# A Mamba-2 and attention trunk on one core: softmax weights turned in 32x32 blocks on VectorE and regrouped through DRAM

## The chip, the core and the metric

One core of one Trainium2 chip runs the whole program. The metric is the device time of one execution in microseconds (us); lower is better. Engines are named as in the profile: PE (TensorE, matrix multiply), PEld (its weight loads), DVE (VectorE), ACT (ScalarE), POOL (GpSimd) and SP (SyncE, which here only issues DMAs). Instructions are said to read "128x512" when 128 partitions hold 512 elements each.

## The reference, cut to what matters

256 positions of width 2048 pass through one Mamba-2 layer, then one causal attention layer with 16 heads of width 128, then a final RMSNorm. Everything is float32.

```python
def reference(x, ...):
    h = rmsnorm(x, a_norm_g)
    x = x + mamba2_layer(h, ...)             # one projection to 10304 columns: z, x, B, C and 64 columns dt
    kb, vb, kbar = shared_kv(x, kv_norm_g, w_kv)
    h = rmsnorm(x, b_norm_g)
    x = x + moba_layer(h, b_w_in, b_w_out, kb, vb, kbar)
    return rmsnorm(x, final_norm_g)

def moba_layer(h, w_in, w_out, kb, vb, kbar):
    proj = h @ w_in                          # 2048 columns of queries, 2048 of gates
    q, z = rope(proj[..., :2048]), proj[..., 2048:]
    o = softmax(causal(q @ k.T * scale)) @ v # per head; 256 positions are one block
    return (o * silu(z)) @ w_out
```

## The kernel before, in words

**The main stream on PE.** All projections are cut into blocks of 512 output columns, and a block into units of 256 input rows. A unit loads a 128x1024 piece of float32 weights (`load`, on SP's queue), splits it into a rounded part `hi` (ACT) and a rest `lo` (DVE, both in `split`), and multiplies: for each of two groups of 128 positions and two groups of 128 input rows three matmuls of 512 columns (`products`), so 12 matmuls in a unit and 96 in a block. They accumulate in four PSUM banks (`ps`). There are 384 such units and one odd one, `dt`, whose weights have 64 columns: 16 pairs of matmuls with the activations as the moving operand, `hi` over 512 columns and `lo` over 256.

**The turn.** A block of queries, gates or convolution channels leaves PSUM with positions on the partitions and is wanted with channels there. `turn` (L385) transposes in 32x32 blocks on DVE (`T`), SP writes `T` to DRAM (`turned`), and four DMAs on POOL's queue read it back regrouped (`U`).

**The side work.** Everything else (convolution, state-space part, norms, attention) is written as Python generators that a planner steps between the products: `some` (L156) takes a step of one whose inputs are due by the planner's own clock, `Side.advance` books when the next is due, and `copied` (L257) books a trip through DRAM as 5.0 us for the write, 0.6 us for each of four issues and 7.0 us for the read. A step is taken only while ACT and DVE stand less than an allowance ahead of PE in that clock: at most 1000 ns, and less near a block's end (`left`, `LAG_END`, `CATCH_UP`). The result is a fixed order on each engine; at run time engines wait only for data.

**Attention.** `att_gen` (L994) handles two heads, eight times in all. It applies rope to the queries, has PE form scores (`K,q`), and on DVE and ACT turns them into normalized weights `E` (tile `Es`, 128x2x384, two buffers), positions on the partitions. The weights must then be transposed: PE does it with the identity, three 128x128 pieces for each head into a PSUM bank `s`, and ACT copies them to `W` (tile `PT`). Four matmuls of `W` with the values follow (`PT,V`), then the gate. The heads come from blocks in the order `z0 q0 z1 q1 z2 q2 q3 z3` (q queries, z gates; L1100). The blocks of the last projection read the gated heads.

**The start and the end.** Before the first data arrive PE runs three 128x512 float32 matmuls on a tile of ones (`warm_up`, L496: one, a 16-column transpose, two). Then `h_gen` transposes x piece by piece, ACT and DVE make the operand `hT`, and the first products follow. At the end `last_evac` (L1134) adds the last products of 128 positions to x, squares, forms the root on 128x1 tiles (`root`, L475), scales four pieces of 512 columns and writes each.

Of the kernel before, what the change touches and what calls it, by code (L numbers as in the profile page):

```python
# [15 lines left out]
P = 128  # L16
L = 256
# [12 lines left out]
LAG = 1000.0  # L30
LAG_END = 0.0
CATCH_UP = 0.3
MARGIN = 750.0
# [98 lines left out]
class Side:  # L132


    def __init__(self, clock, engines, lag):
        self.gens, self.clock, self.engines, self.lag = [], clock, engines, lag

# [3 lines left out]
    def advance(self, entry):  # L141
        gen, ready, _ = entry
        if ready is not None and not ready():
            return 0
        before = [e.ns for e in self.engines]
        at = 0.0
        try:
            entry[1] = next(gen)
            if isinstance(entry[1], float):
                at, entry[1] = entry[1], None  # L150
        except StopIteration:
            self.gens.remove(entry)
        entry[2] = max([e.ns for e, b in zip(self.engines, before) if e.ns > b], default=at)
        return 1

    def some(self, most):  # L156


        PE = self.engines[0]
        for entry in list(self.gens):  # L160
            if most <= 0 or any(e.ns > PE.ns + self.lag() for e in self.engines):
                return
            if entry[2] <= PE.ns - MARGIN:
                most -= self.advance(entry)
# [7 lines left out]
def trunk_kernel(ctx: ExitStack, tc: tile.TileContext, x, a_norm_g, a_w_in, a_conv_w, a_conv_b,  # L172
# [47 lines left out]

    left = [0.0]
    side = Side(clock, [PE, ACT, DVE], lambda: min(LAG, LAG_END + CATCH_UP * (left[0] - PE.ns)))

# [90 lines left out]
    def split(u):  # L314
# [5 lines left out]
        t = RAW.pop(u)  # L320
        shape = [P, 16, 64] if b["form"] == "dt" else [P, 2, 512]
        hi = wts.tile(shape, F32R, name="hi", tag="hi", bufs=HI_BUFS)
        lo = wts.tile(shape, F32R, name="lo", tag="lo", bufs=HI_BUFS)
        HI[u], LO[u] = hi, lo
        if j == 0:
# [17 lines left out]
    def products(u):  # L343
        b, k, row = units[u]
        acc = accs.setdefault(id(b), {})
        hi, lo, k0, k1 = HI.pop(u), LO.pop(u), b["ks"][0], b["ks"][-1]
        last = k + 1 == k1
        if b["form"] == "dt":
            ps = bank("ps_dt")
            for i in range(16):  # L350
                for w, n in ((hi, 2 * L), (lo, L)):
                    PE.matmul(ps[0:64, :n], lhsT=w[:, i, :], rhs=b["operand"](i)[:, :n],
                              start=i == 0 and w is hi, stop=i == 15 and w is lo)
            b["evac"](ps[0:64, :])
            some(4)
            return
        rows = (0, 1) if row is None else (row,)
        for j in rows:
# [15 lines left out]
            some(2)  # L374

    def halves(ps):

        t = take("T")[:ps.shape[0], :L]
        ACT.activation(t, ps[:, L:2 * L], AF.Copy)
        S[0].give((t.tensor.name, t.offset))  # L380
        return ps[:, :L], t

# [109 lines left out]
    early = big.tile([P, 2, 1024], F32, name="early", tag="y6")  # L492
    DVE.memset(early[:, 0, 512:], 1.0)
    warm = take("s")

    def warm_up(n):  # L496
        for _ in range(n):
            PE.matmul(warm, lhsT=early[:, 0, 512:512 + P], rhs=early[:, 0, 512:], start=True, stop=True)

    warm_up(1)  # L500
    g_a = const.tile([P, 16], F32, name="g_a")
# [3 lines left out]
    banks.give((pa.tensor.name, pa.offset))  # L505
    warm_up(2)
    banks.give((warm.tensor.name, warm.offset))
    nt = const.tile([P, 4, 2], F32, name="r0")
# [61 lines left out]
    def dt_evac(ps):  # L570
        a, t = halves(ps)
        w = big.tile([P, 5, L], F32, name="dtw", tag="y7")
        v = w[0:64, 0, :]
        DVE.tensor_add(v, a, t)
        make_room("s")
        p = take("s")[:, :L]
        for i in range(2):
            PE.transpose(p[:, i * P:(i + 1) * P], r0[:, i:i + 1].to_broadcast([P, P]), ident)
        DVE.tensor_mul(v, v, p[0:64])
        give(p)  # L580
        DVE.tensor_scalar(v, v, dta[:, 0:1], None, op0=OP.add)
        side.add(dt_gen(w))

    def dt_gen(w):
# [30 lines left out]
        DVE.tensor_copy(b[64:128, :], a)  # L615
        DVE.tensor_copy(b[0:64, :], dt)
        yield can("s")
        p = take("s")[:, :L].rearrange("p (t c) -> p t c", t=2)
# [375 lines left out]
    def att_gen(half, there, h0):  # L994
# [38 lines left out]
        W = take("PT")  # L1033
        for e in range(2):
            yield can("s")
            T = take("s")[:, :384]
            for i in range(3):
                PE.transpose(T[:, i * P:(i + 1) * P], E[:, e, i * P:(i + 1) * P], ident)
            yield
            ACT.activation(W[:, e, :], T, AF.Copy)  # L1040
            give(T)
        give(E, m)
        yield can("s")
        o = take("s").rearrange("p (e l) -> p e l", e=2)
# [83 lines left out]
    def fin_part():  # L1128

        p = B["p"].tile([P, 2], F32, name="part", bufs=1)  # L1130
        DVE.tensor_reduce(p, ss[:, :, 0:3], axis=mybir.AxisListType.X, op=OP.add)
        B["part"] = p

    def last_evac(ps, t):  # L1134
        if t == 0:
            fin_part()
        v, gf = fin_add(3, t, ps), B["gf"]

        w = B["p"].tile([P, 4, 1], F32, name="sfin", bufs=2)
        DVE.tensor_add(w[:, 0, :], ss[:, t, 3:4], B["part"][:, t:t + 1])  # L1140
        root(w, D)
        r = w[:, 2, :]
        o = B["x1"][t]
        for c in (0, 512):
            ACT.activation(o[:, c:c + 512], o[:, c:c + 512], AF.Copy, scale=r)
        DVE.tensor_scalar(o[:, 1024:1536], o[:, 1024:1536], r, None, op0=OP.mult)
        DVE.scalar_tensor_tensor(v, v, r, gf[:, 1536:], op0=OP.mult, op1=OP.mult)
        for c in (1024, 0, 1536, 512):
            SP.dma_start(dram(out, t * P * D + c, [[D, P], [1, 512]]), o[:, c:c + 512])

# [15 lines left out]
    for i in range(2):  # L1166
        next(prep)
        part(i)
    next(prep)
    load(4)  # L1170
    begun = 1
    for u in range(len(units)):
# [18 lines left out]
        if u == first_p + 12:  # L1191
            open_b()
        rest = (b["ks"][-1] + 1 - k) * (0.32e3 if b["form"] == "dt" else 1.36e3) * (0.5 if b["form"] == "rows" else 1.0)
        left[0] = PE.ns + rest
        products(u)
# [43 lines left out]
```

## Time and profile before

| what | value |
|---|---|
| median of three runs | 1151.7 us (1150.7 to 1152.11) |
| the profiled execution's own time | 1152.41 us |
| its span, first to last instruction | 1150.3 us |
| PE busy | 1137.7 us, 99% |
| DVE, ACT, POOL busy | 835.0 us, 646.7 us, 106.6 us |
| HBM traffic | 232.69 MB read, 18.94 MB written |
| granted TensorE clock, mean | 0.997 of full |

Every wrapped instruction is recorded at one line (L128), so groups are told apart by their tiles: `s<-ident,Es` is a transpose of the weights `Es` into a bank `s`. A matmul's recorded duration contains its pipeline, and the next one begins before it ends; what a matmul costs PE is the distance between starts, which the chain of waits shows. The chain follows the work that ended last back from the end.

### The profile page before, as it was taken

To read this page: it belongs to the slowest core of one execution; us is meant where nothing else is said; L and a number is where in the kernel's file an instruction comes from. 1 tells how busy PE (TensorE), PEld (TensorE's weight loads), DVE (VectorE), ACT (ScalarE), POOL (GpSimd) and SP (SyncE) were. 2 spreads that over 40 slices of the span, in tenths; PEclk is the share of its full clock that TensorE was granted. 3 is DMA by queue.
4 is the path that set the end of the run, shared out by engine and by line. 5 is a ranking of instruction groups with operands and counts; after the bars stand their busy time and mean duration, and the time that the engine had idled before them with its cause. 6 is when DMAs were issued, how large, how long until landed. Compare 5 with 4: busy or idle time off the path is not lost.

```text
span 1150.3 us, 14948 instructions
## 1 busy us (share of the span) xinstructions
PE 1137.7 (99%) x5281; PEld 929.9 (81%) x5281; DVE 835.0 (73%) x1274; ACT 646.7 (56%) x904; POOL 106.6 (9%) x185
## 2 busy tenths in 40 slices
PE   9999999999999999999999999999999999999996
PEld 6778888888888888888878888888888888888885
DVE  5876868787888978787877569876444676677564
ACT  5656566666676566757654655434444354544453
POOL 2011111012011111101000000010000001000000
PEclk9999999999999999999999999999999999999998
DMA  8777879878677778877765457678567677667552
GB/s 261 232 228 218 264 223 282 267 247 256 218 219 238 205 233 237 237 224 234 224 227 168 164 185 234 205 243 257 176 213 229 200 222 227 198 212 239 165 183 91
DMA packets 127674, 252.61 MB, mean 220 GB/s; under 512 B 12336, under 2 KB 12416, under 8 KB 127216
## 3 DMA queue, kind: packets, MB, share of 16 engines
q1 hardware_dynamic: 118080, 222.86, 62.5%
q0 software_dynamic: 9520, 28.81, 9.5%
q8 instruction: 41, 0.67, 0.2%
q14 instruction: 33, 0.27, 0.1%
HBM read 232.69 MB, written 18.94 MB: 219 GB/s over the span
## 4 chain that ended last, share of the span: by engine, by line
PE 99%; DVE 0%; ACT 0%; issue 0%; ACTq 0%
PE ps L128 91%; PE s L128 7%; PE ps_dt L128 0%; ACT hi L128 0%; DVE lo L128 0%; DVE sfin L128 0%; ACT T L128 0%; ACT x L128 0%; DVE x L128 0%; ACTq L1234 0%; DVE dtw L128 0%; DVE early L128 0%; ACT hT L128 0%; ACT sfin L128 0%; DVE ones L128 0%
## 5 line engine op out<-in xcount | busy, mean ns | idle before, releaser
L128 DVE TENSOR_TENSOR lo<-raw,hi 128x1024 fp32r<-128x1024 f32 (+1 forms) x385 | 463.4, 1217 | 196.8 <-ACT hi L128 193.5
L128 ACT ACTIVATE hi<-raw 128x1024 fp32r<-128x1024 f32 (+1 forms) x385 | 397.1, 1052 | 260.1 <-PE ps L128 145.9
L128 PE MATMUL ps<-hi,hT 128*128 128x512 f32 x1280 | 400.7, 394 | 0.7 <-ACT hi L128 0.7
L128 PEld LDWEIGHTS ps<-hi,hT 128*128 128x128 f32 x1280 | 235.7, 188 | 49.2 <-issue 2.2
L128 PE MATMUL ps<-lo,hT 128*128 128x512 f32 x640 | 249.8, 390 | 0.0
L128 PE MATMUL ps<-hi,bop 128*128 128x512 f32 x512 | 160.4, 394 | 0.0
L128 PE MATMUL ps<-hi,yn 128*128 128x512 f32 x512 | 159.7, 393 | 0.0
L128 PE MATMUL ps<-hi,kvop 128*128 128x512 f32 x512 | 158.1, 390 | 0.0
L406 POOL DMA_DIRECT2D U<-turned x128 | 74.1, 586 | 823.1 <-DMA turned<-T 557.2
L128 PEld LDWEIGHTS ps<-lo,hT 128*128 128x128 f32 x640 | 120.1, 188 | 26.4 <-DVE lo L128 0.8
L128 PEld LDWEIGHTS ps<-hi,kvop 128*128 128x128 f32 x512 | 95.8, 188 | 19.7
L128 PEld LDWEIGHTS ps<-hi,bop 128*128 128x128 f32 x512 | 95.1, 188 | 19.1
L128 PEld LDWEIGHTS ps<-hi,yn 128*128 128x128 f32 x512 | 94.6, 188 | 19.0 <-issue 0.3
L128 PE MATMUL ps<-lo,bop 128*128 128x512 f32 x256 | 99.9, 390 | 0.0
L128 PE MATMUL ps<-lo,yn 128*128 128x512 f32 x256 | 99.8, 390 | 0.0
L128 PE MATMUL ps<-lo,kvop 128*128 128x512 f32 x256 | 99.7, 389 | 0.0
L128 PE MATMUL ps<-hi,oop 128*128 128x512 f32 x256 | 80.3, 395 | 0.0
L128 DVE STREAM_TRANSPOSE T<-ps 128x512 f32<-128x512 f32 x64 | 44.4, 708 | 26.6 <-ACT ps L128 17.5
L128 DVE SCALAR_TENSOR_TENSOR xs<-u,cw,xs 128x255 f32<-128x255 f32 (+2 forms) x144 | 59.8, 478 | 0.0
L128 PEld LDWEIGHTS ps<-lo,yn 128*128 128x128 f32 x256 | 48.1, 188 | 10.2
L128 PEld LDWEIGHTS ps<-lo,bop 128*128 128x128 f32 x256 | 48.0, 188 | 10.2
L128 ACT ACTIVATE em<-em,dal 128x128 f32<-128x128 f32 (+1 forms) x128 | 54.4, 449 | 3.0 <-DMA em<-AC 0.9
(167 smaller groups left out, 925.1 us busy)
## 6 DMA issues: line engine op xcount, KB each, us to landing
raw<-in_a_w_in_dram SPq DMA_DIRECT2D x159, 512.0 KB, 4.8
raw<-in_a_w_out_dram SPq DMA_DIRECT2D x64, 512.0 KB, 4.8
raw<-in_w_kv_dram SPq DMA_DIRECT2D x64, 512.0 KB, 4.6
raw<-in_b_w_in_dram SPq DMA_DIRECT2D x64, 512.0 KB, 4.6
turned<-T SPq DMA_DIRECT2D x64, 256.0 KB, 4.3
U<-turned POOLq DMA_DIRECT2D x128, 128.0 KB, 5.9
raw<-in_b_w_out_dram SPq DMA_DIRECT2D x32, 512.0 KB, 4.8
em<-AC POOLq DMA_DIRECT2D x32, 256.0 KB, 5.9
```

Source lines behind the costliest of these rows:

```text
L128: return call(out, *args, **kw)
L406: POOL.dma_start(U[32 * q:32 * q + 32].rearrange("p (b c) -> p b c", b=8), src)
```

## The change

It makes eight edits.

1. `att_gen`: PE's six transposes and ACT's two copies for each pair of heads go. DVE transposes `E` in 32x32 blocks into `W`, SP writes `W` to DRAM (`turned_E`, 384 KB), four DMAs on POOL's queue read it back into `E` in pieces of 768 bytes, and the four matmuls with the values read `E` as moving operand in runs of 32 elements.
2. The blocks' order becomes `z0 q0 q1 z1 q2 q3 z2 z3`.
3. `dt`: `hi` and `lo` stand side by side in one tile (`dtp`), so that 16 matmuls of 512 columns with 128 output partitions do what 32 did; `dt_evac` then adds three parts where it added two.
4. `dt_gen`: the step that follows its two copies is due 3 us after them.
5. `Side`: the allowance is 1000 ns everywhere, and a due time that a generator names counts even where the step has used an engine.
6. The start: the ones are 128 columns (read four times over), and the three warm-up matmuls stand before the 16-column transpose, after it, and behind the first piece of x.
7. The end: the sum's scaling is done once ahead (`fin_part`), the gain is multiplied in while ACT squares, the root takes five small steps on 128x1 tiles, and the pieces are 256, 512, 768 and 512 columns wide, alternating between DVE and ACT.
8. `halves`, which only `dt` used, goes.

```diff
-            if most <= 0 or any(e.ns > PE.ns + self.lag() for e in self.engines):
+            if most <= 0 or any(e.ns > PE.ns + LAG for e in self.engines):
...
-        entry[2] = max([e.ns for e, b in zip(self.engines, before) if e.ns > b], default=at)
+        entry[2] = max([at] + [e.ns for e, b in zip(self.engines, before) if e.ns > b])
...
-            ps = bank("ps_dt")
+            ps, w = bank("ps_dt"), HI.pop(u)
             for i in range(16):
-                for w, n in ((hi, 2 * L), (lo, L)):
-                    PE.matmul(ps[0:64, :n], lhsT=w[:, i, :], rhs=b["operand"](i)[:, :n],
-                              start=i == 0 and w is hi, stop=i == 15 and w is lo)
-            b["evac"](ps[0:64, :])
+                PE.matmul(ps, lhsT=w[:, i, :], rhs=b["operand"](i), start=i == 0, stop=i == 15)
+            b["evac"](ps)
...
-    DVE.memset(early[:, 0, 512:], 1.0)
+    DVE.memset(early[:, 0, 512:512 + P], 1.0)
...
+    def warm_up():
+        w = early[:, 0, 512:512 + P]
+        PE.matmul(warm.rearrange("p (a c) -> p a c", a=4), lhsT=w, rhs=w[:, None, :].to_broadcast([P, 4, P]),
+                  start=True, stop=True)
...
+        yield DVE.ns + 3000.0
         yield can("s")
         p = take("s")[:, :L].rearrange("p (t c) -> p t c", t=2)
...
         yield can("PT")
         W = take("PT")
-        for e in range(2):
-            yield can("s")
-            T = take("s")[:, :384]
-            for i in range(3):
-                PE.transpose(T[:, i * P:(i + 1) * P], E[:, e, i * P:(i + 1) * P], ident)
-            yield
-            ACT.activation(W[:, e, :], T, AF.Copy)
-            give(T)
-        give(E, m)
+        DVE.transpose(W.rearrange("p e l -> p (e l)").rearrange("p (b k l) -> p k b l", b=4, k=6),
+                      E.rearrange("p e (k b l) -> p (e k) b l", k=3, b=4))
+        X = hbm.tile([P, 768], F32, name="turned_E", tag=f"E{h0 // 2 % 2}")
+        SP.dma_start(X, W.rearrange("p e l -> p (e l)"))
+        written = DVE.ns + WRITE
+        freed.append((S[0], (W.tensor.name, W.offset), written))
+        for b in range(4):
+            src = bass.AP(tensor=X.tensor, offset=X.offset + b * 192, ap=[[768, 32], [32 * 768, 4], [1, 192]])
+            POOL.dma_start(E[32 * b:32 * b + 32].rearrange("p e l -> p (e l)").rearrange("p (a c) -> p a c", a=4), src)
+        yield copied(E, written, 4 * 600.0)
+        Wk = E.rearrange("p e l -> p (e l)").rearrange("p (a e k l) -> p e k a l", a=4, e=2, k=3)
+        give(m)
         yield can("s")
         o = take("s").rearrange("p (e l) -> p e l", e=2)
         for e in range(2):
-            PE.matmul(o[:, e, :], lhsT=Vh[e][:, 0, :], rhs=W[:, e, 0:256], start=True, stop=False)
-            PE.matmul(o[:, e, P:L], lhsT=Vh[e][:, 1, :], rhs=W[:, e, 256:384], start=False, stop=True)
-        give(W)
+            PE.matmul(o[:, e, :].rearrange("p (k a l) -> p k a l", k=2, a=4), lhsT=Vh[e][:, 0, :], rhs=Wk[:, e, 0:2],
+                      start=True, stop=False)
+            PE.matmul(o[:, e, P:L].rearrange("p (a l) -> p a l", a=4), lhsT=Vh[e][:, 1, :], rhs=Wk[:, e, 2],
+                      start=False, stop=True)
+        give(E)
...
-    for kind, n in ("z0", "q0", "z1", "q1", "z2", "q2", "q3", "z3"):
+    for kind, n in ("z0", "q0", "q1", "z1", "q2", "q3", "z2", "z3"):
...
+        DVE.scalar_tensor_tensor(m, s, 1.0 / D, B["part"][:, t:t + 1], op0=OP.mult, op1=OP.add)
+        ACT.activation(y, m, AF.Sqrt)
+        DVE.tensor_scalar(h, m, -0.5, None, op0=OP.mult)
+        DVE.reciprocal(y, y)
+        DVE.scalar_tensor_tensor(a, y, h, y, op0=OP.mult, op1=OP.mult)
+        DVE.scalar_tensor_tensor(y, a, 1.5, y, op0=OP.add, op1=OP.mult)
+        for engine, c, e in ((DVE, 0, 256), (ACT, 256, 768), (DVE, 768, 1536), (ACT, 1536, 2048)):
+            if engine is ACT:
+                ACT.activation(o[:, c:e], o[:, c:e], AF.Copy, scale=y)
+            else:
+                DVE.tensor_scalar(o[:, c:e], o[:, c:e], y, None, op0=OP.mult)
+            SP.dma_start(dram(out, t * P * D + c, [[D, P], [1, e - c]]), o[:, c:e])
```

The order of the instructions on an engine changes in three places that matter below.

PE at the very start, before: `early` is the tile of ones, `ga` the 16-column transpose, `xl` a piece of x for 128 positions.

```order
L128 MATMUL s<-early 128x512
L128 MATMUL s<-ident,ga 128x16
L128 MATMUL s<-early 128x512 x2
L128 MATMUL s<-ident,xl_76 128x128
L128 MATMUL s<-ident,xl_77 128x128
L128 MATMUL ps<-hi,hT 128x512 x2
L128 MATMUL ps<-lo,hT 128x512
```

and after the change (the wrapper's line moves from 128 to 126):

```order
L126 MATMUL s<-early 128x512
L126 MATMUL s<-ident,ga 128x16
L126 MATMUL s<-early 128x512
L126 MATMUL s<-ident,xl_76 128x128
L126 MATMUL s<-ident,xl_77 128x128
L126 MATMUL s<-early 128x512
L126 MATMUL ps<-hi,hT 128x512 x2
L126 MATMUL ps<-lo,hT 128x512
```

In both, the transposes of two further pieces of x (four rows like the `xl` rows) stand just before the first products. The third warm-up has moved behind the first piece's transposes.

PE in the attention stage, the first pair of heads, before: the second head's three transposes, 6 products, then the four matmuls with the values.

```order
L128 MATMUL s<-ident,Es 128x128 x3
L128 MATMUL ps<-hi,bop_6148 128x512 x2
L128 MATMUL ps<-lo,bop_6148 128x512
L128 MATMUL s<-PT,V_6412 128x256
L128 MATMUL s<-PT,V_6412 128x128
L128 MATMUL ps<-hi,bop_6149 128x512 x2
```

and after:

```order
L126 MATMUL ps<-hi,bop_6130 128x512 x2
L126 MATMUL ps<-lo,bop_6130 128x512
L126 MATMUL s<-Es,V_6342 128x256
L126 MATMUL s<-Es,V_6342 128x128
L126 MATMUL ps<-hi,bop_6131 128x512 x2
```

The transposes are gone from PE, and the four matmuls (the two `V` rows stand twice in a row in each) come 4 units later in the stream (48 products) than before: they stand 5 to 8 units behind the place where DVE's transpose of the same pair is issued, over the eight pairs.

POOL's queue over the blocks of keys, queries and gates, before and after: `U` are the read-backs of the turn, `Es` those of the weights, `gf` the final gain.

```order
L406 DMA U<-turned 32x8x128 x48
L1123 DMA gf<-in_final_norm_g_dram 128x2048
```

```order
L397 DMA U<-turned 32x8x128 x28
L1036 DMA Es<-turned_E 32x4x192 x8
L397 DMA U<-turned 32x8x128 x4
L1036 DMA Es<-turned_E 32x4x192 x4
L1122 DMA gf<-in_final_norm_g_dram 128x2048
```

Between the last two rows the two kinds alternate until 48 of `U` and 32 of `Es` have gone; a read-back of either kind now stands behind those of the other on this queue.

## Rows read from the trace of the kernel before

**Rows 1.** The page: span, PE's busy time, and the chain's shares by line.

```profile
span 1150.3 us, 14948 instructions
PE 1137.7 (99%) x5281; PEld 929.9 (81%) x5281; DVE 835.0 (73%) x1274; ACT 646.7 (56%) x904; POOL 106.6 (9%) x185
...
PE ps L128 91%; PE s L128 7%; PE ps_dt L128 0%; ACT hi L128 0%; DVE lo L128 0%; DVE sfin L128 0%; ACT T L128 0%; ACT x L128 0%; DVE x L128 0%; ACTq L1234 0%; DVE dtw L128 0%; DVE early L128 0%; ACT hT L128 0%; ACT sfin L128 0%; DVE ones L128 0%
```

**Rows 2.** The chain over the first 60 us: start, duration, work and its count.

```profile
1.01 0.50 DVE early L128
...
1.55 6.36 PE s L128 x9
...
8.00 0.47 ACT hT L128
...
9.05 1.70 PE ps L128 x5
...
10.77 0.50 PE ps L128
...
35.59 5.46 PE ps_dt L128 x32
```

**Rows 3.** PE's timeline at 82 us; in brackets the idle time before.

```profile
82.49 0.44 PE L128 MATMUL s<-ident,dtw 128*128 128x128 f32 x2 [1.03 <-DVE dtw L128]
```

**Rows 4.** The chain in the attention stage.

```profile
920.50 1.31 PE s L128 x8
...
933.40 0.33 PE s L128 x3
933.73 2.09 PE ps L128 x9
...
937.53 1.31 PE s L128 x8
...
947.70 21.81 PE ps L128 x96
```

**Rows 5.** The chain behind the last product.

```profile
1142.56 0.17 DVE sfin L128
...
1144.14 0.72 ACT x L128
```

**Rows 6.** The timeline there: DVE's first piece of the last rows.

```profile
1144.14 0.49 DVE L128 TENSOR_SCALAR x<-x,sfin 128x512 f32<-128x512 f32 x1
```

**Rows 7.** PE's groups, shapes kept apart: count, then busy us and mean ns.

```profile
L128 PE MATMUL s<-ident,Es 128*128 128x128 f32 x48 | 7.8, 272 | 0.0
```

**Rows 8.** Tile U: durations as min/median/max ns, waits on it, DMA landing.

```profile
L406 POOL DMA_DIRECT2D U<-turned x128: 582/582/610, 42.6 to 1051.6; - x128
...
L128 ACT ACTIVATE u<-U x12: 1041/1044/1062, 53.6 to 541.5; 128x1024 f32<-128x1024 f32 x12
L128 ACT ACTIVATE z<-U x8: 1042/1044/1048, 127.0 to 577.0; 128x1024 f32<-128x1024 f32 x8
...
  DVE T L128: 6.4, 3
  ACT u L128: 5.1, 3
...
DMA to landing us min/median/max: 2.6/5.9/9.1
```

**Rows 9.** The timeline of one turn: its last transposes, then POOL's read-backs.

```profile
967.51 1.40 DVE L128 STREAM_TRANSPOSE T<-ps 128x512 f32<-128x512 f32 x2
...
975.23 2.30 POOL L406 DMA_DIRECT2D U<-turned  x4 [23.40 <-DMA turned<-T]
```

**Rows 10.** Windows: busy us of PE, PEld, DVE, ACT, POOL, clock, DMA share, GB/s.

```profile
0.00:5.00 5.00, 3.45 (x5) 1.39 (x6) 0.54 (x2) 1.67 (x3) 4.16 (x13) 1.00 0.45 129
920.00:1080.00 160.00, 160.00 (x763) 133.67 (x762) 115.65 (x219) 79.88 (x144) 14.39 (x25) 1.00 0.70 212
```

**Rows 11.** The page's costliest groups: the turn's transpose on DVE.

```profile
L128 DVE STREAM_TRANSPOSE T<-ps 128x512 f32<-128x512 f32 x64 | 44.4, 708 | 26.6 <-ACT ps L128 17.5
```

More of the change, by code (lines that the diff above doesn't have):

```diff
@@ L30 @@
 LAG = 1000.0
-LAG_END = 0.0
-CATCH_UP = 0.3
 MARGIN = 750.0
@@ L132, with __init__ @@
 class Side:
-    def __init__(self, clock, engines, lag):
-        self.gens, self.clock, self.engines, self.lag = [], clock, engines, lag
+    def __init__(self, clock, engines):
+        self.gens, self.clock, self.engines = [], clock, engines
     def add(self, gen, ready=None):
@@ L219, in trunk_kernel @@
     ctx.enter_context(tc.manual_schedule())
-    left = [0.0]
-    side = Side(clock, [PE, ACT, DVE], lambda: min(LAG, LAG_END + CATCH_UP * (left[0] - PE.ns)))
+    side = Side(clock, [PE, ACT, DVE])
     def of(tag):
@@ L320, in split @@
         t = RAW.pop(u)
[L321 to L324, printed above, removed]
+        if b["form"] == "dt":
+            HI[u] = big.tile([P, 16, P], F32R, name="dtp", tag="y6")
+            hi, lo = HI[u][:, :, :64], HI[u][:, :, 64:]
+        else:
+            hi = wts.tile([P, 2, 512], F32R, name="hi", tag="hi", bufs=HI_BUFS)
+            lo = wts.tile([P, 2, 512], F32R, name="lo", tag="lo", bufs=HI_BUFS)
+            HI[u], LO[u] = hi, lo
         if j == 0:
@@ L345, in products @@
         acc = accs.setdefault(id(b), {})
+        if b["form"] == "dt":
+            ps, w = bank("ps_dt"), HI.pop(u)
+            for i in range(16):
+                PE.matmul(ps, lhsT=w[:, i, :], rhs=b["operand"](i), start=i == 0, stop=i == 15)
+            b["evac"](ps)
+            some(4)
+            return
         hi, lo, k0, k1 = HI.pop(u), LO.pop(u), b["ks"][0], b["ks"][-1]
         last = k + 1 == k1
-        if b["form"] == "dt":
-            ps = bank("ps_dt")
-            for i in range(16):
-                for w, n in ((hi, 2 * L), (lo, L)):
-                    PE.matmul(ps[0:64, :n], lhsT=w[:, i, :], rhs=b["operand"](i)[:, :n],
-                              start=i == 0 and w is hi, stop=i == 15 and w is lo)
-            b["evac"](ps[0:64, :])
-            some(4)
-            return
         rows = (0, 1) if row is None else (row,)
@@ L374, in products @@
             some(2)
[L376 to L381, printed above, removed]
     turned = [0]
@@ L492, in trunk_kernel @@
     early = big.tile([P, 2, 1024], F32, name="early", tag="y6")
-    DVE.memset(early[:, 0, 512:], 1.0)
+    DVE.memset(early[:, 0, 512:512 + P], 1.0)
     warm = take("s")
[L496 to L500, printed above, removed]
+    def warm_up():
+        w = early[:, 0, 512:512 + P]
+        PE.matmul(warm.rearrange("p (a c) -> p a c", a=4), lhsT=w, rhs=w[:, None, :].to_broadcast([P, 4, P]),
+                  start=True, stop=True)
+    warm_up()
     g_a = const.tile([P, 16], F32, name="g_a")
@@ L505, in trunk_kernel @@
     banks.give((pa.tensor.name, pa.offset))
-    warm_up(2)
-    banks.give((warm.tensor.name, warm.offset))
+    warm_up()
     nt = const.tile([P, 4, 2], F32, name="r0")
@@ L570, in dt_evac @@
     def dt_evac(ps):
-        a, t = halves(ps)
         w = big.tile([P, 5, L], F32, name="dtw", tag="y7")
-        v = w[0:64, 0, :]
-        DVE.tensor_add(v, a, t)
+        v, t, t2 = (w[0:64, i, :] for i in range(3))
+        ACT.activation(t, ps[0:64, L:], AF.Copy)
+        DVE.tensor_copy(t2, ps[64:128, :L])
+        DVE.tensor_add(v, ps[0:64, :L], t)
+        DVE.tensor_add(v, v, t2)
         make_room("s")
@@ L1131, in fin_part @@
         DVE.tensor_reduce(p, ss[:, :, 0:3], axis=mybir.AxisListType.X, op=OP.add)
+        DVE.tensor_scalar(p, p, 1.0 / D, EPS, op0=OP.mult, op1=OP.add)
         B["part"] = p
@@ L1136, in last_evac @@
             fin_part()
[L1137 to L1149, printed above, removed]
+        o, gf = B["x1"][t], B["gf"]
+        v = o[:, 1536:]
+        DVE.tensor_add(v, ps, v)
+        make_room("T")
+        sq, w = take("T"), B["p"].tile([P, 5], F32, name="sfin", bufs=2)
+        s, m, h, y, a = (w[:, i:i + 1] for i in range(5))
+        ACT.activation(sq, v, AF.Square, accum_out=s)
+        give(sq)
+        DVE.tensor_mul(v, v, gf[:, 1536:])
+        DVE.scalar_tensor_tensor(m, s, 1.0 / D, B["part"][:, t:t + 1], op0=OP.mult, op1=OP.add)
[7 more added lines that the diff above has]
+                ACT.activation(o[:, c:e], o[:, c:e], AF.Copy, scale=y)
+            else:
+                DVE.tensor_scalar(o[:, c:e], o[:, c:e], y, None, op0=OP.mult)
+            SP.dma_start(dram(out, t * P * D + c, [[D, P], [1, e - c]]), o[:, c:e])
     n_fin = len(blocks)
@@ L1167, in trunk_kernel @@
         next(prep)
+        if not i:
+            warm_up()
         part(i)
     next(prep)
+    banks.give((warm.tensor.name, warm.offset))
     load(4)
@@ L1192, in trunk_kernel @@
             open_b()
-        rest = (b["ks"][-1] + 1 - k) * (0.32e3 if b["form"] == "dt" else 1.36e3) * (0.5 if b["form"] == "rows" else 1.0)
-        left[0] = PE.ns + rest
         products(u)
```

## The prediction

> **What bounds the kernel now.** I read the page first. PE is busy for 1137.7 of 1150.3 us, and the chain that ended last is 91% products and 7% other matmuls, with nothing else above half a per cent [rows 1]. A busy PE alone proves little, since recorded matmuls overlap, so the second view is the chain itself, piece by piece. In the attention stage 96 products take 21.81 us [rows 4], 227 ns each, in an unbroken row; 384 units of 12 such products are 4608 x 0.2272 = 1047 us, which is the 91%. The reader should see that the chain goes straight from one PE piece to the next: PE waits for nobody. So time goes away in three ways only: PE gets less to do, it starts earlier, or less follows its last product. The third view is where it does not run: about 1.5 us before the first matmul, a wait of 1.03 us for the copies in `dt_gen` [rows 3], and the tail behind the last product. DVE is busy 115.65 of 160 us in the attention stage and POOL 14.39 [rows 10], so both have room, and DVE is not the bound.
>
> **The change, part by part.**
>
> *Transposes off PE.* A group of three transposes is 0.33 us of the chain [rows 4], and the stream also pays for the switch: the 9 products behind one take 2.09 us where 9 x 0.2272 = 2.045, some 0.03 us of it the switch as I read it. Sixteen groups (48 instructions [rows 7]) at 0.36 give 5.7 us; where several kinds of small matmul stand together a switch stays, so I take **-5.6 us**. Bounds: 5.3 (no switch) to 5.7.
> The row of these transposes has a mean of 272 ns each [rows 7], and that invites another sum. [...] The trace decides: the 272 ns are latency, three of them fit into 0.33 us of the chain, and only starts cost PE.
>
> *The four matmuls with the values* stay, 1.31 us for a pair [rows 4], but their moving operand now lies in runs of 32 elements. No matmul of the trace before reads so. The nearest rows are on ACT: reading `U` in 32-element runs (`u`) takes a median of 1044 ns for 1024 elements, reading it straight (`z`) 1044 [rows 8]. So I take 0. If PE read such runs at half rate, eight pairs would cost 8 x 1.31 = 10.5 us; a gain has no reason. Bounds 0 to +10.5.
>
> *dt.* 32 matmuls are 5.46 us of the chain [rows 2]; 16 of 512 columns at 0.2272 are 3.64. **-1.8 us**. The extra copy and addition in `dt_evac` lie on ACT and DVE. The two transposes that waited 1.03 us [rows 3] now stand three units further back in the stream, 3 x 2.73 = 8.2 us (a unit is 21.81 / 8), while the copies move by a step or two at most: **-1.0 us**, bounds 0 and 1.03.
>
> *The start.* The chain says the warm-ups set the first transposes of x: one piece of 6.36 us from 1.55 to 7.9, then ACT, then the first products at 9.05 and the last early break at 10.77 [rows 2]. That piece holds six halves of the three warm-ups and three small transposes; with about 1 us for the small ones each warm-up is near 1.8 us; the filling of the ones takes 0.50 and would take about 0.35 less for a quarter of the columns. Without one warm-up in front, the transposes could begin 1.8 + 0.35 = 2.1 us earlier, near 5.2. The data allow it: in the first 5 us 129 GB/s arrived [rows 10], 0.64 MB, and the first two pieces of x are 0.52 MB at the head of SP's queue. But the third warm-up now stands before the second piece's transposes, which therefore run near 7.3; then hT on ACT (0.47), the split of the second half of the weights on ACT and on DVE, and the last early break comes near 9.6 instead of 10.77. **-1.1 us**. Bounds 0 (the weights arrive too late to use it) and 2.1.
>
> *The end.* From the sum of squares (1142.56) to the scale factor (1144.14) the chain has eight small steps, 1.6 us [rows 5]; five remain at the same 0.2 each, saving 0.5 to 0.6. The first piece on DVE, 0.49 us for 512 columns [rows 6], becomes one of 256, at some 0.3, and the writes start by that much earlier. **-0.7 us**, bounds 0.3 and 1.0.
>
> *What is added elsewhere.* Eight DVE transposes of 768 elements, by the turn's 708 ns for 512 [rows 11] about 1.06 us each, 8.5 us in a stage where DVE has 44 us free; splits run three units ahead of PE, which covers one transpose. Should that cover go, each would delay PE by at most its 1.06 us. POOL issues 32 more DMAs at 582 ns [rows 8], 18.6 us beside 14.39 of 160. DMA moves 6.3 MB more in 160 us, 39 GB/s on top of 212: a share of 0.70 becomes about 0.83. On SP the eight writes wait for their DVE transpose with loads behind them, but those loads wait for later DVE splits anyway. On POOL read-backs of both kinds queue behind each other; each holds the queue for 2.3 us plus the wait for its write.
>
> *The new wait.* The four matmuls now wait for a trip through DRAM: DVE's transpose, a write, four issues, a read. The turn makes the same trip. In the slowest turn of the stage that I found, DVE ended at 968.9 and POOL could issue at 975.23, 6.3 us later [rows 9]; the fourth issue follows 1.7 us on, and a read lands in 2.6 to 9.1 us, median 5.9 [rows 8]: 14.0 us. The matmuls stand 5 to 8 units behind the transpose, 13.6 us or more, plus what other small matmuls stand between, and DVE tends to run ahead of that place. So most trips are hidden. Of 32 turns six made DVE or ACT wait, 11.5 us in all [rows 8], 0.36 us per trip, and eight trips at that rate are 2.9 us. But those engines reach their place ahead of PE, so I take **+0.4 us**; bounds 0 and 15.6 (below).
>
> *Free edits.* The new order of blocks puts two blocks (2 x 21.81 us) between the last queries and the last projection instead of one, more than the trip adds. The fixed allowance lets DVE or ACT stand 1 us further ahead at a block's end and so free its banks later; the next user of a bank comes at least two units (5.4 us) later, which hides that.
>
> Sum: -5.6 - 1.8 - 1.0 - 1.1 - 0.7 + 0.4 = **-9.8 us**. The profiled execution took 1152.4 us, which gives 1142.6; the median of the runs shown is 0.7 below it, and for a median I say **1141.9 us**.
>
> **The rivals.**
>
> *A. Data bind the start.* If the first weights (0.52 MB behind x, at the same rate some 3 us later) come only when the third warm-up is over, nothing is gained: 1143.0. For it: DMA moves only 129 GB/s in the first 5 us; against: before, ACT began the first split right behind hT, with no wait for data in the chain.
>
> *B. Read-backs are sometimes late.* At the turn's 2.9 us instead of 0.4: 1144.4. For it: both kinds share POOL's queue, and a write of 384 KB is half again the turn's. Against: the planner books 14.4 us, more than the slowest turn above.
>
> *C. Read-backs are late each time, slower than before.* The place is PE before the four matmuls of each pair. At the worst rows, 6.3 us for the write, 1.7 of issues and 9.1 for the landing are 17.1 us against the 15.15 that the planner grants (14.4 and 0.75 of margin): 1.95 us for each of eight, 15.6 in all, gives 1141.9 - 0.4 + 15.6 = 1157.1. It decides against the change once the mean wait passes (9.8 + 0.4) / 8 = 1.3 us. Against it: it takes the worst of both transfers each time, and POOL's 128 issues never took above 610 ns [rows 8].
> [...]
>
> *D. PE reads the runs at half rate.* 1141.9 + 10.5 = 1152.4, no change within measurement. Against it stands ACT's equal pair of rows.
>
> *E. The change doesn't do what it says on PE:* the order is new everywhere, and if the dt wait returns and small waits of the kind in [rows 3] come at two or three further places, 1.0 us each: 1146.
>
> **How the numbers follow.** The forecast 0.66, A 0.10, B 0.13, C 0.03, D 0.03, E 0.05. About 0.2% (2.3 us) is what a measurement can tell from no change. Forecast, A, B and E are faster by more: 0.94; I take 0.01 off for a mixture of B and D that ends slower. Faster 0.93, same 0.03 (D), slower 0.04 (C and that). Range: below, every gain at its bound, 5.7 + 1.8 + 1.0 + 2.1 + 1.0 = 11.6, gives 1140.1, and 0.5 for the runs' spread 1139.6; above, B and E and one more such wait, 1147.0. C, D and the rest of A to E beyond it stay out.
>
> **What would show it.** Right: no `ident,Es` on PE; the chain still all PE in the attention stage, about 5.6 us shorter there; `dt` near 3.64 us; no wait at `dtw`; first products 1 us earlier; 0.7 us less behind the last product; four-matmul groups still 1.31 us. Wrong: idle time on PE before `s<-Es,V` released by a DMA (B, C), those groups near 2.6 us (D), an early break still near 10.8 us (A), or new idle on PE released by DVE or ACT (E).

## The result, and the profile after

| what | before | after |
|---|---|---|
| median of four runs | 1151.37 us (1150.7 to 1152.11) | 1144.43 us (1143.61 to 1146.1) |
| ratio of the medians, 95% interval | | 0.9944 (0.9932 to 0.9955) |
| the profiled execution's own time | 1152.41 us | 1143.61 us |
| its span | 1150.3 us | 1141.9 us |

The kernel is 6.9 us faster by the medians. The two profiled executions lie 8.8 us apart, their spans 8.4: the one of before is 1.0 above its median, the one of after is the fastest of its four, 0.8 below it. What follows takes the spans apart first, and comes to the 1.9 us between the two readings at the end. One of the five runs of experiment 8's kernel with before's start took 1629.75 us at a mean granted clock of 0.654, so its median and ratio there are those of the other four.

The page of after, as [rows 1]: PE loses 64 matmuls and 7.6 us of busy time, POOL gains 32 issues, and the chain is still PE's, but for 1% that now waits for a load.

```profile
span 1141.9 us, 14900 instructions
PE 1130.1 (99%) x5217; PEld 923.2 (81%) x5217; DVE 839.2 (73%) x1283; ACT 641.6 (56%) x890; POOL 124.4 (11%) x217
...
PE ps L126 90%; PE s L126 6%; DMA raw<-in_a_w_in_dram 1%; PE ps_dt L126 0%; DVE xs L126 0%; DVE lo L126 0%; ACT hi L126 0%; SPq L416 0%; DVE x L126 0%; DVE T L126 0%; SPq L306 0%; ACT T L126 0%; ACT x L126 0%; DVE sfin L126 0%; ACTq L1243 0%
```

All of PE's waits in the whole run of after (us in total, times, longest). There are three, all in the first 20 us. No `dtw` [rows 3] and no `Es` is among them.

```profile
PE s L126 <- DVE early L126: 1.2, 1, 1.2
PE s L126 <- DMA xl<-in_x_dram: 0.5, 1, 0.5
PE ps L126 <- ACT hi L126: 0.4, 1, 0.4
```

The chain over the first 60 us of after, as [rows 2]. It no longer begins with the warm-ups: it waits until 13.40 for a piece of the first weights, and from that landing to `dt` it is one unbroken row.

```profile
4.78 8.62 DMA raw<-in_a_w_in_dram
...
13.41 1.07 ACT hi L126
...
14.51 1.22 DVE lo L126
15.73 0.61 DVE early L126 x2
16.34 0.41 DVE hT L126
...
16.79 0.73 PE ps L126 x2
...
35.42 3.63 PE ps_dt L126 x16
```

The chain in the attention stage and behind the last product of after, as [rows 4, 5]. The pieces of three transposes are gone, a pair's four matmuls with the values (944.89, eight records) still take 1.31.

```profile
917.71 1.31 PE s L126 x8
...
922.41 22.48 PE ps L126 x99
944.89 1.31 PE s L126 x8
...
1065.83 66.70 PE ps L126 x294
...
1132.55 0.70 DVE x L126
...
1133.33 0.73 ACT T L126 x2
...
1134.09 0.69 DVE x L126
1134.78 0.08 DVE sfin L126
...
1135.76 0.72 ACT x L126
```

The timeline of after: the first and the slowest of the eight new trips, from DVE's transpose to POOL's four read-backs, as [rows 9] for the turn. The read-backs can be issued 4.9 and 8.1 us behind the transpose's end.

```profile
928.64 0.97 DVE L126 STREAM_TRANSPOSE PT<-Es 128x768 f32<-128x768 f32 x1
...
934.52 2.19 POOL L1036 DMA_DIRECT2D Es<-turned_E  x4 [9.30 <-DMA turned_E<-PT]
...
974.63 0.97 DVE L126 STREAM_TRANSPOSE PT<-Es 128x768 f32<-128x768 f32 x1
...
983.68 2.19 POOL L1036 DMA_DIRECT2D Es<-turned_E  x4 [7.72 <-DMA turned_E<-PT]
```

Of the tile `Es`, the read-backs' durations in ns and their landing, as [rows 8] for `U`; then the window of [rows 10] (columns as there).

```profile
L1036 POOL DMA_DIRECT2D Es<-turned_E x32: 551/553/646, 934.5 to 1056.3; - x32
...
DMA to landing us min/median/max: 2.2/3.6/7.8
```

```profile
920.00:1080.00 160.00, 160.00 (x738) 133.65 (x737) 123.35 (x229) 76.43 (x132) 32.07 (x57) 1.00 0.85 259
```

Where the 8.4 us of the spans went, place by place:

| place | before | after | difference | forecast |
|---|---|---|---|---|
| `dt` begins | 35.59 | 35.42 | -0.2 | -1.1 |
| `dt` takes | 5.46 | 3.63 | -1.8 | -1.8 |
| wait at `dtw` | 1.03 | none | -1.0 | -1.0 |
| first scores to the last product's end | 920.50 to 1140.99 | 917.71 to 1132.53 | -5.7 | -5.6 |
| last product's end to the scale factor's first use | 3.1 | 3.2 | +0.1 | -0.7 |
| waits for the read-back | | none | 0 | +0.4 |

They sum to -8.6; between the end of `dt` and the first scores after takes 0.2 us longer, which gives the 8.4. Against the forecast of -9.8 the start and the end are missing, 1.7 us together, and the 0.4 set aside for read-backs was not needed.

### The profile page after: what moved, and what is told of

The parts are those of the page before. It is cut to its first block, busy times and chain, and to the rows that moved or that the text cites. A ratio compares the mean times of both kernels' runs of the same rounds, so it can differ in the third digit from the quotient of the medians.

```text
span 1141.9 us, 14900 instructions
## 1 busy us (share of the span) xinstructions
PE 1130.1 (99%) x5217; PEld 923.2 (81%) x5217; DVE 839.2 (73%) x1283; ACT 641.6 (56%) x890; POOL 124.4 (11%) x217
## 4 chain that ended last, share of the span: by engine, by line
PE 96%; DMA 1%; DVE 1%; ACT 0%; SPq 0%; issue 0%; ACTq 0%; DVEq 0%
PE ps L126 90%; PE s L126 6%; DMA raw<-in_a_w_in_dram 1%; PE ps_dt L126 0%; DVE xs L126 0%; DVE lo L126 0%; ACT hi L126 0%; SPq L416 0%; DVE x L126 0%; DVE T L126 0%; SPq L306 0%; ACT T L126 0%; ACT x L126 0%; DVE sfin L126 0%; ACTq L1243 0%
```

## The experiments

In the expectations T is the theory that the two traces led to, R a rival, each put for the run at hand. Before was run beside each; its number stands in brackets.

**1. The end, the gain's product in a tile of its own.** In after's timeline ACT squares 512 columns of `x`, and DVE multiplies the gain into the same columns.

```profile
1133.33 0.63 ACT L126 ACTIVATE T<-x 128x512 f32<-128x512 f32 x1 [2.96 <-DVE x L126]
...
1134.09 0.69 DVE L126 TENSOR_TENSOR x<-x,gf 128x512 f32<-128x512 f32 x1 [0.85 <-ACT T L126]
```

The product overwrites what the square reads, so it waits for it, and the small steps wait behind it on DVE.

```diff
-        DVE.tensor_mul(v, v, gf[:, 1536:])
+        g = big.tile([P, 512], F32, name="vg", tag=f"y{1 + t}")
+        DVE.tensor_mul(g, v, gf[:, 1536:])
...
-                ACT.activation(o[:, c:e], o[:, c:e], AF.Copy, scale=y)
+                ACT.activation(o[:, c:e], g if c == 1536 else o[:, c:e], AF.Copy, scale=y)
```

> The changed kernel, with the gain at the end multiplied into a tile of its own instead of in place. Theory T (the in-place multiply has to wait until ACT's Square has read the same elements): DVE's multiply moves beside the Square, the factor is ready 0.6 to 0.7 us earlier, and from the last product to the first scaled piece it takes 2.5 to 2.6 us instead of 3.2; the span is 0.6 us shorter if the rest falls out alike. Rival R (the end already has what there is to gain; the chain of small steps sets it): the same 3.2 us.

Measured: 1142.67 us (1150.22), span 1141.0. The two now run side by side, in the timeline and then in the chain:

```profile
1133.01 0.63 ACT L126 ACTIVATE T<-x 128x512 f32<-128x512 f32 x1 [3.51 <-DVE x L126]
1133.01 0.69 DVE L126 TENSOR_TENSOR vg<-x,gf 128x512 f32<-128x512 f32 x1
```

```profile
1133.77 0.17 DVE sfin L126
...
1134.84 0.72 ACT x L126
```

The last product ended at 1132.26, so the factor is used 2.58 us later instead of 3.24: 0.66 less, the forecast's 0.7 almost to the digit once the wait is gone. It is no accident of one execution: with the tile the stretch is 2.58 us again in the profile of experiment 8's second kernel (1131.64 to 1134.22). The whole time of one run does not show it, and so it was timed again:

> The kernel with the gain multiplied into its own tile at the end, timed. The one profile of it had 0.66 us less behind the last product. Theory T: 0.6 to 0.7 us faster than the changed kernel in the median, which is near what the runs' spread hides: between 0 and 1.3 us. Rival R: no difference.

Measured, five runs: 1144.31 us (1141.51 to 1144.76; before 1151.1), ratio 0.9934 (0.9921 to 0.9946). The spread of 3 us hides 0.66. Inconclusive by the time; the gain is read from the tail alone.

**2. The start as before.** The ones are 512 columns again, and the warm-ups stand as one and two around the 16-column transpose.

```diff
-    DVE.memset(early[:, 0, 512:512 + P], 1.0)
+    DVE.memset(early[:, 0, 512:], 1.0)
...
-    warm_up()
+    warm_up(2)
...
-        if not i:
-            warm_up()
```

> The changed kernel with the start of before (512 columns of ones, one warm-up, the small transpose, two warm-ups). Theory T (the loads set the pace of the first 17 us, so what the start gains is lost again): the first product comes 1.5 us later, at 9.0 us, but the first dt matmul within 0.3 us of the changed kernel's 35.26. Rival R (the start is worth the 1.1 us forecast): the first dt matmul 1 us later or more, about 36.4.

Measured: 1144.09 us (1150.22), span 1142.4. In the chain of this run the first products come at 7.84, and `dt` begins 0.9 us *earlier* than with the new start:

```profile
1.56 5.15 PE s L126 x9
...
7.84 1.69 PE ps L126 x5
...
34.52 3.62 PE ps_dt L126 x16
```

Both theories miss: T had the first products at 9.0 and `dt` within 0.3 us of the new start, R had `dt` 1 us later. The chain's piece of warm-ups and small transposes, 6.36 us in [rows 2], is 5.15 here, with the same instructions. PE's timelines, of before and then of this run, show where (a warm-up is recorded as two halves, so these are the last two warm-ups):

```profile
3.77 3.78 PE L128 MATMUL s<-early 128*128 128x512 f32 x4
```

```profile
3.78 2.70 PE L126 MATMUL s<-early 128*128 128x512 f32 x4
```

The first two halves take 2.07 and 2.08 us in the two runs. With the new start the last two halves take 1.02 us in after and 1.92 in experiment 4. So the same work goes at about half pace in PE's first microseconds, and the moment at which the pace doubles differs between executions (what sets it, no run here tells), although the windows state a granted clock of 1.00 throughout. The length on which the start's term was worked out scatters by over 1 us with it.

What else sets the start shows when runs are put side by side. In six runs, one of them with the old start (experiment 7), the chain begins with the load of the same piece of weights, and `dt` starts a fixed time behind its landing:

| run | landing | `dt` begins | apart |
|---|---|---|---|
| after | 13.40 | 35.42 | 22.0 |
| experiment 1, first run | 13.13 | 35.14 | 22.0 |
| before with the fixed allowance (experiment 7) | 13.04 | 35.06 | 22.0 |
| after without the 3 us (experiment 3) | 12.80 | 34.81 | 22.0 |
| experiment 1, timed | 12.53 | 34.53 | 22.0 |
| parameters later (experiment 8) | 12.34 | 34.37 | 22.0 |

After's second profile (experiment 5) fits, with the landing at 13.50. The landing so scatters by 1.2 us, and the old start meets it as well as the new one: `dt` begins in PE's timeline between 34.36 and 35.34 in six profiles with the new start and the parameters as in after, and between 34.36 and 35.43 in five with the old one. The new start is worth nothing that these profiles can show.

**3. `dt_gen` without the due time of 3 us.**

```diff
-        yield DVE.ns + 3000.0
```

> The changed kernel without the 3 us that dt_gen waits after its two copies; PE's two transposes of dtw stand one unit earlier. Theory T (three units of the move, two of them from the other edits, already cover the copies): no wait, a cost within 0.1 us. Rival R (the 3 us are what removed the wait): PE waits again for DVE at these transposes, 0.5 to 1.0 us.

Measured: 1143.67 us (1150.22). PE's timeline shows the `dtw` transposes without a wait, 3.3 us ahead of where they stand in after (87.40):

```profile
84.07 0.38 PE L126 MATMUL s<-ident,dtw 128*128 128x128 f32 x2
```

The wait of [rows 3] goes without this edit, as T had it. The order of blocks is not what removes it either: with the old order (experiment 6) there is no wait at `dtw`, and none in before with edit 1 and the rule on due times alone. Of what that run shares with after, only the rule on due times concerns this place; it was not tried by itself.

**4. The trip booked 4 us shorter,** so that the four matmuls stand nearer to the transpose. It takes the cover away that the forecast counted on.

```diff
-        yield copied(E, written, 4 * 600.0)
+        yield copied(E, written, 4 * 600.0) - 4000.0
```

> The changed kernel with the trip of the softmax weights booked 4.0 us shorter, so that the four matmuls with the values stand 1 to 4.5 units earlier and follow DVE's transpose by some 10.4 us of the planner's clock. Theory T (trips end 10 to 15 us after the transpose, and the booking hides them): PE now waits before some of the eight groups for the read-back, 1 to 3 us each where it does and 2 to 8 us in all. Rival R (there is slack of 4 us and more everywhere): no wait of PE on the read-back, the span unchanged within 0.5 us.

Measured: 1158.3 us (1150.22), 14.5 above after's second timing (1143.82, below). PE's waits and then the windows around one of them (busy us of PE, PEld, DVE, ACT, POOL, granted clock, DMA share, GB/s):

```profile
PE s L126 <- DMA Es<-turned_E: 9.0, 2, 5.2
```

```profile
973.00:978.00 5.00, 1.24 (x5) 0.80 (x4) 1.55 (x2) 1.06 (x1) 2.31 (x4) 0.79 1.03 287
978.00:982.00 4.00, 4.00 (x12) 3.27 (x12) 1.46 (x2) 0.63 (x1) 0.63 (x2) 0.50 1.06 320
```

and the chain there:

```profile
971.27 6.20 DMA Es<-turned_E
...
977.61 2.90 PE s L126 x8
```

Only two of the eight pairs wait, 9.0 us in all, but the kernel loses 14.5. Behind the wait the granted clock is 0.50 (978 to 982), and the eight matmuls take 2.90 us instead of 1.31, behind both waits; the products that follow are slow too until it rises again (51 of them take 12.69 us here, the first 50 behind the second wait 12.54, together some 2.3 more than at 0.2272 each). Waits of 9.0, twice 1.59 and 2.3 make the 14.5. A wait of PE costs about 1.6 times itself here, and the waits alone are more than the 2 to 8 us that T gave the run. So a booking 4 us below the planner's 15.15 us is too short, and C of the forecast is kept away by the booking.

**5. The old allowance in the changed kernel,** with after timed again beside it.

```diff
-            if most <= 0 or any(e.ns > PE.ns + LAG for e in self.engines):
+            if most <= 0 or any(e.ns > PE.ns + self.lag() for e in self.engines):
```

> The changed kernel once more, unaltered, as the reference for the two timed runs beside it. Its runs shown so far spread over 2.5 us (1143.6 to 1146.1). Theory T (small waits of PE in the state-space stage that come in some executions and not in others): a spread of 1 to 2.5 us again, and if the profile falls on a slower execution, PE idle before transposes of `squares` or products of `xs` near 99, 235 or 304 us. Rival R (a constant cost): runs within 0.7 us of each other.

> The changed kernel with the allowance of before (less side work near the end of a block, at most 1000 ns). Theory T (the fixed allowance costs nothing on the path, as forecast): the same median as the changed kernel within 1 us. Rival R (the fixed allowance lets ACT and DVE fall behind, which makes the small waits of PE near 304 us): 1 us or more faster, and no such waits in the profile. A third way: the old allowance pushes steps of attention later (the last four-matmul groups stand three units further back) and is slower by some us.

Measured: after, five runs, 1143.82 us (1142.76 to 1144.79), ratio 0.9935 (0.9922 to 0.9949); with the old allowance, four runs, 1163.98 us (1163.02 to 1165.14), ratio 1.0111 (1.0097 to 1.0124), so 20.2 us slower than after and 12.9 slower than before (1151.1). PE's timeline shows where most of it goes:

```profile
623.84 0.66 PE L128 MATMUL s<-ident,squares 128*128 128x128 f32 x2 [3.44 <-DVE squares L128]
...
627.49 0.66 PE L128 MATMUL s<-ident,nt 128*128 128x128 f32 x2 [2.98 <-DVE nt L128]
...
631.07 0.80 PE L128 MATMUL ps<-hi,yn 128*128 128x512 f32 x1 [2.92 <-ACT yn L128]
```

```profile
615.00:640.00 25.00, 15.20 (x63) 10.73 (x62) 11.64 (x30) 5.42 (x6) 0.00 (x0) 0.73 0.24 81
```

These are the last norm of the Mamba layer, 300 us ahead of the attention. With the tighter allowance the planner puts off its steps until the blocks that read its result force them, DVE and ACT are late, and PE stands three times in a row, at a granted clock of 0.73. In the written order the norm's last transposes come in unit 204 here, near 200 and 201 in after, 200 and 202 in before. Neither theory had it. The same kernel also waits 2.3 us for a read-back `Es`, with the trip booked in full.

**6. The old order of blocks, and the trip alone.** The first keeps all of after but the order `z0 q0 z1 q1 z2 q2 q3 z3`; the second is before with edit 1 and the rule on due times of edit 5, and nothing else.

```diff
-    for kind, n in ("z0", "q0", "q1", "z1", "q2", "q3", "z2", "z3"):
+    for kind, n in ("z0", "q0", "z1", "q1", "z2", "q2", "q3", "z3"):
```

> The changed kernel with the query and gate blocks in the order of before (z0 q0 z1 q1 z2 q2 q3 z3). In its program the last pair's four matmuls stand one unit before the products that need that pair's heads. Theory T (the new order is what makes room for the trip): PE waits near the last projection for read-backs and for the gated heads, 8 to 20 us in all, and the granted clock falls behind the waits, so that the whole is slower than before. Rival R (the order costs nothing, as the prediction's free edit): within 1 us of the changed kernel.

> The kernel before with the softmax weights' trip through DRAM alone (and the booking of due times that it needs); order of blocks, allowance, dt, start and end as before. Theory T (the trip takes 5.7 us off PE but needs the new order of blocks): the last pair's four matmuls stand one unit before the products that need those heads, PE waits there as in the run with the old order, and the kernel ends within 3 us of the kernel before, either side. Rival R (the trip alone carries the gain): 5 us or more faster than before.

Measured, one timed execution each: 1151.52 us and 1155.32 us (1151.36). The old order takes 7.7 us from the changed kernel, all of its gain, though T's 8 to 20 us of waits did not come; the trip by itself is 4.0 us *slower* than before, though PE has 48 transposes less; T's bound of 3 us is passed by 1. PE's waits with the old order, then those with the trip alone, and the latter's window:

```profile
PE ps L126 <- ACT oop L126: 2.7, 2, 1.4
...
PE ps L126 <- DVE oop L126: 0.8, 2, 0.6
```

```profile
PE ps L128 <- ACT oop L128: 2.8, 2, 1.4
PE s L128 <- DMA Es<-turned_E: 2.1, 3, 1.1
```

```profile
1055.00:1063.00 8.00, 6.08 (x24) 4.41 (x23) 7.30 (x17) 4.06 (x6) 0.00 (x0) 0.90 0.81 233
```

`oop` is the gated heads, the operand of the last projection. With one block between the last queries and that projection, the last pair's four matmuls stand right ahead of the products that need its result; with two blocks, as in after, they do not. The waits for `oop` are 3.5 us with the old order, and the granted clock in the 6 us from 1086, where the last two of them end, is 0.72; what makes up the rest of the 7.7 us was not taken apart.

**7. The fixed allowance in before.**

```diff
-    side = Side(clock, [PE, ACT, DVE], lambda: min(LAG, LAG_END + CATCH_UP * (left[0] - PE.ns)))
+    side = Side(clock, [PE, ACT, DVE], lambda: LAG)
```

> The kernel before with the fixed allowance of 1000 ns alone. Theory T (with the earlier dt of the kernel before, neither allowance makes PE wait, so the forecast's zero holds for this edit against the kernel before, and the 20 us that the old allowance costs in the changed kernel come from its dt standing later): within 1.5 us of before. Rival R (the fixed allowance is worth time by itself): 2 us faster or more. A third way: it is slower by itself.

Measured: 1151.46 us (1151.36). Nothing, and the `dtw` wait is still there with 0.7. The 20.2 us of experiment 5 are therefore no general worth of the allowance: in before the tight one does no harm, in the changed kernel it does. With which of the other edits it does so is not shown. The rule on due times is not enough: before with that rule, the trip and the tight allowance (experiment 6) has none of the three waits of experiment 5.

**8. Towards a faster kernel.** Two versions of after with the tile of experiment 1: one with before's start, one with the new start and POOL's eight small parameter loads held back until the first piece's split (some 7 us), to leave the queues to x and the weights (DVE then first clears a column or two in each of their tiles).

```diff
-    for src, n in ((a_conv_b, 48), (a_gnorm_g, 32), (kv_norm_g, 16), (b_norm_g, 16)):
-        POOL.dma_start(vec[row:row + n, :], dram(src, 0, [[P, n], [1, P]]))
...
         part(i)
+        if not i:
+            load_parameters()
```

> The changed kernel with the gain in its own tile at the end and with the start of before. Theory T (loads bind the first 17 us, the old start loses nothing, and the end brings 0.66 us): the same median as the kernel with the new end alone within 0.7 us; dt starts between 34.3 and 35.4 us. Rival R (the new start is worth 1 us): 1 us slower than the kernel with the new end alone.

> The changed kernel with the gain in its own tile at the end, and with POOL's eight small loads of parameters held back until the first weights are split (about 7 us), so that they no longer share the first 7 us with x and the first weights. Theory T (loads bind the start): the first pieces of x come earlier, PE waits less for them, and dt starts 0.3 to 1.0 us before the 34.98 of the kernel with the new end alone. Rival R (the pace of ACT and DVE binds the start, not the loads): dt starts at 35 us as before, within 0.2.

Measured, five runs each beside the same before (1151.36): 1143.25 us with before's start (1142.44 to 1144.4), ratio 0.9928 (0.9915 to 0.9942), so the old start is not slower than the new one (1144.31 in experiment 1), against R; 1142.05 us with the later parameters (1141.31 to 1143.21), ratio 0.9919 (0.9905 to 0.9932). The second is the fastest kernel of the study, 9.3 us ahead of before and, by the medians, 1.8 to 2.4 ahead of after, whose interval its own overlaps or touches. That the parameters are the reason is not shown: its `dt` begins at 34.37, at the lower edge of the scatter above, and one profile can't tell a new mean from luck. The first version's profile has a wait that after's has not:

```profile
1065.15 1.11 PE L126 MATMUL s<-Es,V 128*128 128x256 f32 x5 [1.14 <-DMA Es<-turned_E]
```

## Why the prediction was right or wrong

The direction and the size held: 1144.43 us lies in the range, faster by 0.56%, on the side that had 0.93. The forecast of 1141.9 was 2.5 us too low. Two slips in the working change nothing there: the range's upper end, "B and E and one more such wait", adds up to 1149.5 (2.5, 4.1 and 1.0 over 1141.9) and not to 1147.0, and 0.52 MB at 129 GB/s takes 4 us and not 3.

- *Transposes off PE*: right. 5.7 us against 5.6. What counted was their spacing on the chain, 0.33 for three, not the 272 ns of a record [rows 7]: 48 x 0.272 would have been 13.
- *Runs of 32 elements*: right, no cost. The chain's groups stay at 1.31 us, and by shapes the 256-column matmul takes 381 ns on `Es` against 379 on `PT` in before. D falls.
- *dt and its wait*: right, 1.8 and 1.0. The reason was half right: the place did move, but neither edit 4 (experiment 3) nor the order of blocks (experiment 6) was needed for the wait to go.
- *The start*: wrong, and this is the term that failed: "-1.1 us", worked out from one chain's warm-ups, measured as 0.2 in the two profiles and as nothing over the eleven of experiment 2. The first transposes of x did come near 5.2 (5.24) and the first products 1.5 us earlier (7.52 for 9.05), but then rival A's data bound: the piece of weights that lands at 13.40 starts all that follows, by 22.0 us in six runs. Before's chain [rows 2] has PE as the bound in an execution with long warm-ups; with the same start in experiment 7 they were short, and the load bound there too. The price of 1.8 us for a warm-up was that of the slow pace; the one that was moved took 0.86 us of PE in after (6.21 to 7.07).
- *The end*: the mechanism was right, the term of -0.7 was mis-sized to +0.1. The five steps are shorter, but I had the gain's multiplication "while ACT squares" and did not see that it writes what the square reads. In a tile of its own it gives 0.66.
- *The read-back*: +0.4 forecast, none in this profile. The slowest time from transpose to issue was 8.1 us against the 6.3 of [rows 9], longer, but the read landed in 3.6 us (median) against 5.9, so that the trip fitted. It does not fit in every execution: with the trip booked in full PE waits once for 1.1 us in experiment 8, once for 2.3 in experiment 5 with the old allowance, and three times, 2.1 in all, with the trip alone in experiment 6, which is B's kind. C, a wait in each pair, comes in none of these profiles. C was priced too low, though: at the mean wait of 1.1 us for eight pairs (9.0 / 8), under its "1.3", experiment 4 was already 8.1 us slower than before. The short issues that stood against it (at most 610 ns, [rows 8]) came again: 32 took 551 to 646 ns each, while DVE was busy 123.35 of 160 us.
- *Free edits*: zero against before is right for the allowance (experiment 7), but neither is free within the change. Without the new order 7.7 us are lost, without the allowance 20.2. The order's reason, two blocks for one, held (experiment 6); the allowance I argued from banks at a block's end alone, and it decides at the last norm of the Mamba layer, 300 us ahead of the attention. They don't add to the sum: they keep it.
- *The median*: of the 2.5 us, 1.0 is the terms above (1142.6 was forecast for the profiled execution, 1143.61 measured). The other 1.5 come from which executions were profiled: I took 0.7 off for a before above its median, and after's profile fell 0.8 below its own. By the profiled executions the gain is 8.8, and after timed again gives 7.3 (1151.1 to 1143.82) and here 6.9. Profiles of nearly the same program show PE waits that others lack: 0.4 for `xs` in after's second profile, 1.6 at 304 us in experiment 2, 1.1 at 1065 for a read-back in experiment 8. That such waits make the slower executions of after was not shown, since each profile is of another execution; it is B in small, at the price of single waits.

## What to carry to other kernels

Where PE is never idle, what leaves its stream is worth its spacing on the chain (three transposes 0.33 us, where a record of one is 0.272), and it is worth that only if nobody else becomes late: here the same trip alone cost 4.0 us, and with the order and the allowance that give it room it brought 5.7. A term for the start or the end needs the next bound behind the one that is removed (the landing of the weights; the buffer that two engines share), and a start read from a single execution may be off by 1 us. A stall of PE of some us can cost more than its own length where the granted clock falls behind it (9.0 us of waits cost 14.5 in experiment 4); behind one of 1.1 us in experiment 8 the next five matmuls took 1.11 us, as in after without a wait (1.10).

## What the runs showed of the hardware

- In 5 us in which PE was busy for 1.24, with one wait of 3.76, the granted clock was 0.79, then 0.50 in the next 4 us, and eight matmuls took 2.90 us instead of 1.31 (experiment 4). Nine us of waiting became 14.5. Behind the single wait of 1.1 us in experiment 8 the next five matmuls took 1.11 us, the same five in after 1.10. With the old order (experiment 6) the clock was 1.00 in the 6 us from 1054, in which PE was busy for 4.13, and 0.72 in the 6 us from 1086, in which it was busy for 5.39.
- The same nine instructions at the start took 6.36 and 5.15 us in two executions, at a granted clock of 1.00 in the profile's windows: four halves of warm-ups took 3.78 and 2.70. The landing of the same load lay between 12.34 and 13.50.
- A matmul's moving operand in runs of 32 float32 elements was as fast as a straight one (381 and 379 ns for 256 columns).
- A read-back of 96 KB in pieces of 768 bytes landed in 3.6 us (median) beside a DMA share of 0.85, in 4.5 in the profile of experiment 4; one of 128 KB in the turn took 6.2 in the same stretch of the first.
